# The last six lower products of an MLP stage issued as twelve of 256 columns

## Chip, cores and metric

The kernel runs on one core of one Trainium2 chip. The metric is the device time of one execution in microseconds (us). The kernel before was timed three times: 345.19 us is the median, 344.91 and 346.03 are the ends. Times within a run are read from one profiled execution.

## What is computed

A decoder block on 256 tokens of width 1024, all in float32: a gated mixer (causal pooling and attention), and then an MLP with a squared ReLU. The change lies in the MLP, which holds the last half of the time:

```python
u2 = rmsnorm(h, norm_mlp_pre[l])
a = jnp.square(jax.nn.relu(u2 @ w_up[l]))          # 1024 -> 4096
h = h + rmsnorm(a @ w_down[l], norm_mlp_post[l])   # 4096 -> 1024
```

## The kernel before

Every float32 operand of a product is split into a high part of type float32r and a low part, the rest (`split_hi` L87 on ScalarE, `split_lo` L91 on VectorE or GpSimd). A product of two operands is then three TensorE products: high by high, high by low, low by high. Each of them is a weight load of a 128x128 block (the stationary operand, read by PEld in the profile) and a stream of 256 or 512 columns (the moving operand, PE in the profile) that adds into a bank of PSUM. A bank holds 512 float32 columns.

The hidden width of 4096 is cut into eight chunks of 512. For each chunk there is an **upper part** and a **lower part**:

- The upper part of chunk j (`up_half` L794, called twice) computes `u2 @ w_up` for 512 hidden units. The weights `up_h`, `up_l` are stationary; the tokens `u2h`, `u2l` move, 256 columns at a time. Each call of `up_half` issues 2 x 8 x 3 = 48 products through `mm3` (L223; its three products are L227, L228 and L229), so an upper part has 96 products of 256 columns. Squared ReLU and the split of its result into `ah`, `al` follow on ScalarE and VectorE.
- The lower part of chunk j multiplies that result by the chunk's 512 rows of `w_down`. Here the tokens `ah`, `al` are stationary and the weights `dn_h`, `dn_l` move, 512 columns at a time. `mm3_wide` (L231) issues six products for one token tile t and one block k of 128 rows: for each of two banks the high tokens by `dn_h` (L236) and by `dn_l` (L237), and then for both banks the low tokens by `dn_h` (L240). Two token tiles and four blocks make 8 x 6 = 48 products of 512 columns. They accumulate in the four banks `pd` over all chunks.

The order on TensorE is written out by hand in program order; nothing reorders it. Upper parts 0 and 1 come first. In upper part 1 each call of `up_half` stands behind four 128x128 transposes (`up_turned`, tile `ut_ps`). Then the loop at L870 runs over j: lower part j, the splits of the next blocks of weights (`split_next(2)` L876), and upper part j + 2 while there is one. So the order is lower 0, upper 2, lower 1, upper 3, ..., lower 5, upper 7, lower 6, lower 7. Six upper parts (2 to 7) stand directly behind a lower part; lower 6 is followed by lower 7. `finish` (L844) ends each token tile.

Other stretches of the program matter for comparison, since they too consist of products of 256 columns through `mm3`: the feature products of the mixer (tiles `q_ps`, `k_ps`, `p_ps`, `g_ps`, 48 products per bank), the scores (`s_ps`, L512 and L513), the pooling projection (`y_ps`, six products a time) and the two branch products (`bp_ps` and `ba_ps`, 24 products a time, turn by turn, L701).

Of the kernel before, what the change touches and what calls it, by code (L numbers as in the profile page):

```python
# [17 lines left out]
D = 1024  # L18
S = 256
NT = S // P  # L20
# [13 lines left out]
def hybrid_block(ctx: ExitStack, tc: tile.TileContext, x, norm_mix_pre, w_in, b_gate, pool_w, pool_scale,  # L34
# [4 lines left out]
    nc = tc.nc  # L39
# [10 lines left out]
    def bank(name):  # L50
        return psum.tile([P, 512], F32, tag="bank", name=name)
# [83 lines left out]
    bu, bd = [None] * NCH, [None] * NCH  # L135
# [18 lines left out]
    def split_next(n=1):  # L154
        for _ in range(n):
            if done[1] < len(order):
                b = next_block()
                b.split(b in shared)
                load_next()
# [71 lines left out]
    def mm3_wide(pss, xhl, whl, start, stop):  # L231

        (xh, xl), (wh, wl) = xhl, whl
        for n, ps in enumerate(pss):
            c = slice(n * 512, (n + 1) * 512)
            nc.tensor.matmul(ps, xh, wh[:, c], start=start, stop=False, skip_group_check=True)  # L236
            nc.tensor.matmul(ps, xh, wl[:, c], start=False, stop=False, skip_group_check=True)  # L237
        for n, ps in enumerate(pss):
            c = slice(n * 512, (n + 1) * 512)
            nc.tensor.matmul(ps, xl, wh[:, c], start=False, stop=stop, skip_group_check=True)  # L240

    def tokens(hl, k, t):
        c = slice(t * P, (t + 1) * P)
        return hl[0][:, k, c], hl[1][:, k, c]

    def wide(blocks, k):
        b = blocks[k // 2]
        return b.hi[:, k % 2, :], b.lo[:, k % 2, :]
# [478 lines left out]
    def out_proj(t, ks, pss, n=None):  # L727
        for k in ks:
            if n is None:
                mm3_wide(pss, tokens(m, k, t), wide(bo, k), k == 0, k == KD - 1)  # L730
            else:
                h, l = wide(bo, k)
                c = slice(n * 512, (n + 1) * 512)
                mm3(pss[n], tokens(m, k, t), (h[:, c], l[:, c]), k == 0, k == KD - 1)
# [36 lines left out]
    def up_parts(j):  # L771
        return tuple(work.tile([P, 4, S], F32R, tag=f"a{i}", name=f"a{i}{j}") for i in "hl")
# [21 lines left out]
    def up_half(j, f2, a):  # L794
        ps = bank(f"up_ps{j}_{f2}")
        for i in range(2):
            cs = slice((2 * f2 + i) * P, (2 * f2 + i + 1) * P)
            for k in range(KD):
                mm3(ps[:, i * S:(i + 1) * S], narrow(bu[j], k, cs), (u2[0][:, k, :], u2[1][:, k, :]),
                    k == 0, k == KD - 1)  # L800
        if f2 == 0:
            split_next(2)
        q = two(squared_relu(ps, f"{j}_{f2}"))
        parts(a[0][:, 2 * f2:2 * f2 + 2, :], a[1][:, 2 * f2:2 * f2 + 2, :], q)
# [36 lines left out]
    pd = [[bank(f"d_ps{t}{n}") for n in range(2)] for t in range(NT)]  # L841
# [27 lines left out]
    prev, nxt = a0, a1  # L869
    for j in range(NCH):  # L870
        last = j == NCH - 1
        for t, k in [(t, k) for t in range(NT) for k in range(4)]:
            if last and t == NT - 1:
                continue
            mm3_wide(pd[t], tokens(prev, k, t), wide(bd[j], k), j == 0 and k == 0, last and k == 3)
        split_next(2)  # L876
        if last:
            break
        if j + 2 < NCH:
            a = up_parts(j + 2)  # L880
            up_half(j + 2, 0, a)
            up_half(j + 2, 1, a)
        else:
            a = None
        prev, nxt = nxt, a
# [35 lines left out]
```

## Time and profile before

| what | us |
|---|---|
| median of three runs | 345.19 |
| the profiled execution | 345.76 |
| its span, from the first to the last instruction | 344.0 |
| PE busy in the span | 334.4 |
| lower part 0, from 181.23 to 192.13 | 10.90 |
| upper part 2, from 192.13 to 203.44 | 11.31 |
| lower part 1, from 203.44 to 214.31 | 10.87 |

The rows of a timeline have the start in us, the duration in us, the engine, the line, the operation and its operands as output<-inputs, sizes, and a count where rows are merged. Inputs of a matmul are named in an order that does not tell which one moves. The durations of products overlap: a product of 256 columns is shown with 0.28 us and one of 512 columns with 0.39 us, while the next one starts long before that has passed. What a product costs in a dense stream is therefore read from the distance of two starts, which is called the **pitch** here. In a view of windows, each row has the stretch, its length, and the busy time of each engine in it, with the number of instructions that touch it in brackets.

### The profile page before, as it was taken

Reading aid. Unit: us, or ns where it says so; the run is one execution under the profiler, and the core shown is the slowest. Engines: PE = TensorE matmul, PEld = TensorE weight load, DVE = VectorE, ACT = ScalarE, POOL = GpSimd, SP = SyncE. Lnnn points to the kernel's source line nnn. Section 1 sums busy time; section 2 is a strip of 40 time slices with the busy share of each in tenths; the row PEclk is TensorE's granted clock in tenths of the full one; section 3 lists DMA queues with packets and bytes.
Section 4 is the critical chain, followed back from the end, with each engine's and each line's share of the span. In section 5 each row is a group of like instructions: output and inputs, shape, how many; then the busy total and the mean of one; then the engine's idle time right before and its main releaser. Section 6 shows DMA issues by size and latency. Waiting matters only on the chain.

```text
span 344.0 us, 5679 instructions
## 1 busy us (share of the span) xinstructions
PE 334.4 (97%) x2313; PEld 309.1 (90%) x2313; DVE 220.5 (64%) x288; ACT 182.3 (53%) x257; POOL 77.3 (22%) x70
## 2 busy tenths in 40 slices
PE   7999999999999999999999999999999999999991
PEld 6799999999999999888898998989989889899880
DVE  2899698996476689376677736547366373653545
ACT  3895658765656755175767435354273451644231
POOL 3699965144303000046600000000000000000000
PEclk9999999999999999999999999999999999999998
DMA  6988761654455946707364854908539166090003
GB/s 203 386 283 282 165 229 32 231 160 157 174 177 193 364 131 229 253 2 245 122 189 179 310 180 163 325 2 274 216 100 328 62 247 243 35 327 9 0 0 122
DMA packets 27506, 63.04 MB, mean 183 GB/s; under 512 B 1332, under 2 KB 3160, under 8 KB 27480
## 3 DMA queue, kind: packets, MB, share of 16 engines
q1 hardware_dynamic: 26904, 62.15, 52.3%
q0 software_dynamic: 576, 0.52, 1.0%
q8 instruction: 18, 0.29, 0.4%
q14 instruction: 8, 0.07, 0.1%
HBM read 61.10 MB, written 1.05 MB: 181 GB/s over the span
## 4 chain that ended last, share of the span: by engine, by line
PE 93%; DVE 2%; DMA 2%; ACT 2%; SPq 0%; issue 0%; DVEq 0%; ACTq 0%
PE up_ps L227 9%; PE up_ps L229 9%; PE up_ps L228 9%; PE d_ps L236 8%; PE d_ps L237 8%; PE d_ps L240 8%; PE g_ps L227 4%; PE g_ps L228 4%; PE g_ps L229 4%; PE wo_ps L236 2%; PE wo_ps L240 2%; PE wo_ps L237 2%; DMA x_sb<-in_x_dram 2%; PE q_ps L227 1%; PE bp_ps L228 1%; PE bp_ps L227 1%
## 5 line engine op out<-in xcount | busy, mean ns | idle before, releaser
L227 PE MATMUL up_ps<-u2h,up_h 128*128 128x256 f32 x224 | 63.0, 281 | 0.0
L228 PE MATMUL up_ps<-u2l,up_h 128*128 128x256 f32 x224 | 62.8, 280 | 0.0
L229 PE MATMUL up_ps<-u2h,up_l 128*128 128x256 f32 x224 | 62.8, 280 | 0.0
L93 DVE TENSOR_TENSOR dn_l<-dn_r,dn_h 128x2048 fp32r<-128x2048 f32 x16 | 36.5, 2291 | 16.5 <-ACT dn_h L89 16.4
L236 PE MATMUL d_ps<-dn_h,ah 128*128 128x512 f32 x120 | 46.7, 389 | 0.0
L237 PE MATMUL d_ps<-dn_l,ah 128*128 128x512 f32 x120 | 46.7, 389 | 0.0
L229 PEld LDWEIGHTS up_ps<-u2h,up_l 128*128 128x128 f32 x224 | 42.9, 191 | 0.0
L228 PEld LDWEIGHTS up_ps<-u2l,up_h 128*128 128x128 f32 x224 | 42.1, 188 | 0.2
L227 PEld LDWEIGHTS up_ps<-u2h,up_h 128*128 128x128 f32 x224 | 42.1, 188 | 0.2
L89 ACT ACTIVATE dn_h<-dn_r 128x2048 fp32r<-128x2048 f32 x16 | 30.4, 1914 | 21.4 <-issue 12.8
L863 POOL TENSOR_TENSOR o_out<-o_out,g_mlp_post 128x256 f32<-128x256 f32 x2 | 1.5, 729 | 165.5 <-DVE rr L295 161.4
L240 PE MATMUL d_ps<-dn_h,al 128*128 128x512 f32 x120 | 36.9, 389 | 0.0
L227 PE MATMUL g_ps<-uh,g_h 128*128 128x256 f32 x128 | 36.1, 282 | 0.0
L228 PE MATMUL g_ps<-ul,g_h 128*128 128x256 f32 x128 | 35.7, 279 | 0.0
L229 PE MATMUL g_ps<-uh,g_l 128*128 128x256 f32 x128 | 35.7, 279 | 0.0
L93 DVE TENSOR_TENSOR up_l<-up_r,up_h 128x2048 fp32r<-128x2048 f32 (+1 forms) x14 | 30.2, 2193 | 8.1 <-ACT up_h L89 8.1
L776 ACT ACTIVATE relu<-up_ps 128x512 f32<-128x512 f32 x16 | 9.5, 594 | 41.5 <-PE up_ps L229 41.5
L778 DVE TENSOR_TENSOR a<-up_ps,relu 128x512 f32<-128x512 f32 x16 | 11.0, 690 | 30.9 <-ACT relu L776 30.8
L89 ACT ACTIVATE up_h<-up_r 128x2048 fp32r<-128x2048 f32 x16 | 29.9, 1904 | 1.6 <-PE wo_ps L240 1.6
L240 PEld LDWEIGHTS d_ps<-dn_h,al 128*128 128x128 f32 x120 | 22.5, 188 | 4.7
L237 PEld LDWEIGHTS d_ps<-dn_l,ah 128*128 128x128 f32 x120 | 22.5, 188 | 4.4
L236 PEld LDWEIGHTS d_ps<-dn_h,ah 128*128 128x128 f32 x120 | 22.5, 188 | 4.4
(225 smaller groups left out, 836.7 us busy)
## 6 DMA issues: line engine op xcount, KB each, us to landing
up_r<-in_w_up_dram SPq DMA_DIRECT2D x16, 1024.0 KB, 5.6
dn_r<-in_w_down_dram SPq DMA_DIRECT2D x16, 1024.0 KB, 5.5
g_r<-in_w_in_dram SPq DMA_DIRECT2D x8, 1024.0 KB, 5.5
o_r<-in_w_out_dram SPq DMA_DIRECT2D x4, 1024.0 KB, 4.8
v_r<-in_w_in_dram SPq DMA_DIRECT2D x8, 256.0 KB, 5.7
q_r<-in_w_in_dram SPq DMA_DIRECT2D x4, 512.0 KB, 6.2
k_r<-in_w_in_dram SPq DMA_DIRECT2D x2, 1024.0 KB, 5.5
p_r<-in_w_in_dram SPq DMA_DIRECT2D x2, 1024.0 KB
```

Of the source, the lines that this page charges most:

```text
L89: nc.scalar.activation(self.hi[:, s, :], self.raw[:, s, :], AF.Copy)
L93: eng.tensor_tensor(self.lo[:, s, c], self.raw[:, s, c], self.hi[:, s, c].bitcast(F32), ALU.subtract)
L227: nc.tensor.matmul(ps, wh, rh, start=start, stop=False, skip_group_check=True)
L228: nc.tensor.matmul(ps, *second, start=False, stop=False, skip_group_check=True)
L229: nc.tensor.matmul(ps, *third, start=False, stop=stop, skip_group_check=True)
L236: nc.tensor.matmul(ps, xh, wh[:, c], start=start, stop=False, skip_group_check=True)
L237: nc.tensor.matmul(ps, xh, wl[:, c], start=False, stop=False, skip_group_check=True)
L240: nc.tensor.matmul(ps, xl, wh[:, c], start=False, stop=stop, skip_group_check=True)
L776: nc.scalar.activation(r, ps, AF.Relu)
L778: nc.vector.tensor_tensor(a, ps, r, ALU.mult)
L863: nc.gpsimd.tensor_tensor(o[:, 768:D], o[:, 768:D], g_mlp_post[:, 768:D], ALU.mult)
```

## The change

In lower parts 0 to 6, the last of the eight calls of `mm3_wide` (token tile 1, block 3) is replaced by a new function, `mm3_quarters`. It covers the same columns with the same operands in pieces of 256 columns: for each of four pieces the high tokens by `dn_h` and by `dn_l`, and then for the four pieces the low tokens by `dn_h`.

```diff
+    def mm3_quarters(pss, xhl, whl):
+
+        (xh, xl), (wh, wl) = xhl, whl
+        pieces = [(pss[c // 512][:, c % 512:c % 512 + 256], slice(c, c + 256)) for c in range(0, D, 256)]
+        for ps, c in pieces:
+            nc.tensor.matmul(ps, xh, wh[:, c], start=False, stop=False, skip_group_check=True)
+            nc.tensor.matmul(ps, xh, wl[:, c], start=False, stop=False, skip_group_check=True)
+        for ps, c in pieces:
+            nc.tensor.matmul(ps, xl, wh[:, c], start=False, stop=False, skip_group_check=True)
...
         for t, k in [(t, k) for t in range(NT) for k in range(4)]:
             if last and t == NT - 1:
                 continue
-            mm3_wide(pd[t], tokens(prev, k, t), wide(bd[j], k), j == 0 and k == 0, last and k == 3)
+            if not last and (t, k) == (NT - 1, 3):
+
+                mm3_quarters(pd[t], tokens(prev, k, t), wide(bd[j], k))
+            else:
+                mm3_wide(pd[t], tokens(prev, k, t), wide(bd[j], k), j == 0 and k == 0, last and k == 3)
```

On TensorE, at the seam between lower part 0 and upper part 2, the order before is this (numbers in names tell buffers and banks apart; `d_ps` are the lower banks, `up_ps` an upper bank):

```order
L236 MATMUL d_ps_2195<-dn_2_h,ah_1733 128x512
L237 MATMUL d_ps_2195<-dn_2_l,ah_1733 128x512
L236 MATMUL d_ps_2196<-dn_2_h,ah_1733 128x512
L237 MATMUL d_ps_2196<-dn_2_l,ah_1733 128x512
L240 MATMUL d_ps_2195<-dn_2_h,al_1734 128x512
L240 MATMUL d_ps_2196<-dn_2_h,al_1734 128x512
L227 MATMUL up_ps_0_2260<-u2h,up_0_h 128x256
L228 MATMUL up_ps_0_2260<-u2l,up_0_h 128x256
L229 MATMUL up_ps_0_2260<-u2h,up_0_l 128x256
```

The same place on TensorE after the change:

```order
L247 MATMUL d_ps_2195<-dn_2_h,ah_1733 128x256
L248 MATMUL d_ps_2195<-dn_2_l,ah_1733 128x256
L247 MATMUL d_ps_2195<-dn_2_h,ah_1733 128x256
L248 MATMUL d_ps_2195<-dn_2_l,ah_1733 128x256
L247 MATMUL d_ps_2196<-dn_2_h,ah_1733 128x256
L248 MATMUL d_ps_2196<-dn_2_l,ah_1733 128x256
L247 MATMUL d_ps_2196<-dn_2_h,ah_1733 128x256
L248 MATMUL d_ps_2196<-dn_2_l,ah_1733 128x256
L250 MATMUL d_ps_2195<-dn_2_h,al_1734 128x256 x2
L250 MATMUL d_ps_2196<-dn_2_h,al_1734 128x256 x2
L227 MATMUL up_ps_0_2266<-u2h,up_0_h 128x256
L228 MATMUL up_ps_0_2266<-u2l,up_0_h 128x256
```

Nothing moved: six rows became twelve products in the same place (the last two rows stand for two products each), and the upper part now stands behind products of 256 columns. The seventh place, the end of lower part 6 on TensorE, has no upper part behind it; after the change it reads:

```order
L247 MATMUL d_ps_2196<-dn_26_h,ah_3024 128x256
L248 MATMUL d_ps_2196<-dn_26_l,ah_3024 128x256
L250 MATMUL d_ps_2195<-dn_26_h,al_3025 128x256 x2
L250 MATMUL d_ps_2196<-dn_26_h,al_3025 128x256 x2
L236 MATMUL d_ps_2193<-dn_28_h,ah_3214 128x512
L237 MATMUL d_ps_2193<-dn_28_l,ah_3214 128x512
```

There the twelve pieces are followed by the products of 512 columns of lower part 7. The other engines and the DMA queues have the same instructions in the same order as before.

## Prediction

> **What bounds the kernel now.** The page comes first: the span, the busy times, and the chain that ended last; then the view of waits for TensorE alone.
>
> ```profile
> span 344.0 us, 5679 instructions
> PE 334.4 (97%) x2313; PEld 309.1 (90%) x2313; DVE 220.5 (64%) x288; ACT 182.3 (53%) x257; POOL 77.3 (22%) x70
> PE 93%; DVE 2%; DMA 2%; ACT 2%; SPq 0%; issue 0%; DVEq 0%; ACTq 0%
> ```
>
> ```profile
> PE x_ps L306 <- DMA x_sb<-in_x_dram: 1.0, 1, 1.0
> PE busy L61 <- PEq L907: 0.8, 1, 0.8
> ```
>
> 93% of the chain is TensorE, and its only listed waits (1.0 and 0.8 us) lie at the start of the program. So the MLP costs what its products cost, each at its pitch, and every nanosecond of pitch goes straight into the time. The windows of the MLP show the parts one by one: the second call of upper part 1, lower part 0, upper part 2, lower part 1.
>
> ```profile
> 175.68:181.23 5.55, 5.55 (x51) 5.55 (x50) 4.85 (x4) 2.67 (x5) 0.00 (x0) 1.00 0.56 185
> 181.23:192.13 10.90, 10.90 (x51) 9.02 (x49) 8.56 (x15) 7.96 (x10) 0.00 (x0) 1.00 0.48 163
> 192.13:203.44 11.31, 11.31 (x98) 11.31 (x97) 5.40 (x4) 3.15 (x3) 0.00 (x0) 1.00 0.91 329
> 203.44:214.31 10.87, 10.87 (x50) 9.01 (x49) 6.40 (x5) 6.75 (x5) 0.00 (x0) 1.00 0.32 106
> ```
>
> PE is busy for the whole of each, at granted clock 1.00. Lower part 1 is 48 products in 10.87 us: 226.5 ns each. Upper part 2 is 96 products in 11.31 us: 117.8 ns each. The 48 products of the second call in upper part 1 took 5.55 us, 115.6 ns each, though they have the same shape, the same tokens and the same kind of weights. The timeline says why: the first rows below are the end of that call, then the start of lower part 0.
>
> ```profile
> 179.87 0.28 PE L227 MATMUL up_ps<-u2h,up_h 128*128 128x256 f32 x1
> ...
> 181.23 0.39 PE L236 MATMUL d_ps<-dn_h,ah 128*128 128x512 f32 x1
> ...
> 182.16 0.39 PE L240 MATMUL d_ps<-dn_h,al 128*128 128x512 f32 x1
> ```
>
> From 179.87 to 181.23 stand twelve products: 1.36 us, or **113.3 ns** each, half of the 226.5 of a product with twice the columns. Upper part 2 never gets there; its rows begin behind the last two lower products:
>
> ```profile
> 191.68 0.61 PE L240 MATMUL d_ps<-dn_h,al 128*128 128x512 f32 x2
> 192.13 0.28 PE L227 MATMUL up_ps<-u2h,up_h 128*128 128x256 f32 x1
> 192.25 0.28 PE L228 MATMUL up_ps<-u2l,up_h 128*128 128x256 f32 x1
> 192.36 0.28 PE L229 MATMUL up_ps<-u2h,up_l 128*128 128x256 f32 x1
> ...
> 203.32 0.28 PE L229 MATMUL up_ps<-u2h,up_l 128*128 128x256 f32 x1
> 203.44 0.39 PE L236 MATMUL d_ps<-dn_h,ah 128*128 128x512 f32 x1
> ```
>
> From the first row to the last it keeps 117 to 118 ns, as do the other five that follow a lower part. So a dense stream of 256 columns has **two steady pitches, 113.3 and 117.8 ns**, and which one holds is decided where the stream begins. The transposes ahead of upper part 1 let it in at the fast one; products of 512 columns let it in at the slow one, six times out of six. DMA traffic does not separate them, as the four windows in the next fence show: fast at 294 and 404 GB/s, slow at 111 and 298.
>
> **The change part by part.** What decides is how a 256-column stream begins when another stands ahead of it without a gap. The mixer has such seams. First windows: `g_ps` behind scores, `g_ps` behind the pooling projection, `ba_ps` behind `bp_ps`, `bp_ps` behind `ba_ps` (48, 48, 24 and 24 products); then the seam of the third of these in the timeline.
>
> ```profile
> 59.01:64.47 5.46, 5.46 (x51) 1.00 0.94 294
> 94.94:100.60 5.66, 5.66 (x51) 1.00 0.38 111
> 115.45:118.18 2.73, 2.73 (x26) 1.00 1.02 404
> 118.18:121.01 2.83, 2.83 (x27) 1.00 0.75 298
> ```
>
> ```profile
> 115.34 0.28 PE L229 MATMUL bp_ps<-yh,bp_l 128*128 128x256 f32 x1
> 115.45 0.28 PE L227 MATMUL ba_ps<-oTh,ba_h 128*128 128x256 f32 x1
> 115.57 0.28 PE L228 MATMUL ba_ps<-oTl,ba_h 128*128 128x256 f32 x1
> 115.69 0.28 PE L229 MATMUL ba_ps<-oTh,ba_l 128*128 128x256 f32 x1
> 115.80 0.28 PE L227 MATMUL ba_ps<-oTh,ba_h 128*128 128x256 f32 x1
> 115.91 0.28 PE L228 MATMUL ba_ps<-oTl,ba_h 128*128 128x256 f32 x1
> ```
>
> That is 113.8, 117.9, 113.8 and 117.9 ns each: `ba_ps` changes from the long pitch to the short one within three products (2.73 us against 24 x 113.3 = 2.72: 0.01 us to settle), and `g_ps` behind scores at 5.46 against 48 x 113.3 = 5.44 (0.02). I counted all fifteen such seams in the timeline: seven lead to 113.3 (scores behind `k_ps`, `p_ps` behind scores, `g_ps` behind scores, and all four `ba_ps`), eight to 117.8 or more (`g_ps` and `y_ps` behind each other twice each, `bp_ps` four times). Of the three kinds that were slow ahead of the seam and whose follower also runs fast somewhere, two went fast (`ba_ps`; `g_ps` behind scores) and one stayed slow (`g_ps` behind `y_ps`).
>
> *Removed and added.* Seven calls lose 6 products of 226.5 ns (1.36 us) and get 12 of 256 columns, with 6 more weight loads each. A load stands beside the product ahead of it: in the lower windows PEld is busy 9.02 of 10.90 us, in the upper ones throughout, and PE is without a gap in both. At 113.3 ns the twelve cost 1.36 us: nothing lost. At 117.8 ns, 1.41: 0.05 a call. The slowest dense rows of this shape are the six of `y_ps` and the scores ahead of `g_ps`:
>
> ```profile
> 57.01 0.36 PE L512 MATMUL s_ps<-stacked 128*128 128x256 f32 x1
> 59.01 0.29 PE L227 MATMUL g_ps<-uh,g_h 128*128 128x256 f32 x1
> ...
> 100.60 0.28 PE L227 MATMUL y_ps<-ys_pws 128*128 128x256 f32 x1
> ...
> 101.32 0.28 PE L227 MATMUL g_ps<-uh,g_h 128*128 128x256 f32 x1
> ```
>
> `y_ps` is 6 in 0.72 us, 120 ns each; at that, the twelve cost 1.44, or 0.08 a call. Seven calls: 0 to +0.57 us. I take 117.8, the row nearest to it, since 256 columns directly behind 512 have run so six times: **+0.38 us**.
>
> The Trainium skill speaks against pieces: Perfetto Trace Analysis, section Matmuls, says that larger matmuls are more efficient than smaller ones. TensorE: Matmul & The Clock Gate, section Back-to-back issue gap, puts the warm gap at N / 2.4 + 2.5 ns; by that, an estimate from the page, each of 42 halved products would cost 2.5 ns more, 0.11 us in all. Here 2 x 113.3 against 226.5 shows no such fixed cost at the short pitch, and 2 x 117.8 a larger one (9 ns) at the long one.
>
> *Upper parts 2 to 7.* At the fast pitch: 96 x 113.3 = 10.88 us, plus 0.02 to settle, plus the way back into 512 columns: the four products from 181.23 to 182.16 took 0.93 us against 4 x 226.5 = 0.91, another 0.02, which lower parts 1 to 6 would now pay. 11.31 − 10.92 = 0.39 us, six times: **−2.34 us**.
>
> *The other engines* keep their order. A shorter upper part is only worth its time if the next weights are split by then. Rows of VectorE, and the PE row that they must be ahead of:
>
> ```profile
> 207.52 4.50 DVE L93 TENSOR_TENSOR up_l<-up_r,up_h 128x2048 fp32r<-128x2048 f32 x2 [1.11 <-ACT up_h L89]
> 214.31 0.28 PE L227 MATMUL up_ps<-u2h,up_h 128*128 128x256 f32 x1
> 216.69 2.29 DVE L93 TENSOR_TENSOR dn_l<-dn_r,dn_h 128x2048 fp32r<-128x2048 f32 x1 [0.60 <-ACT dn_h L89]
> 225.62 0.39 PE L236 MATMUL d_ps<-dn_h,ah 128*128 128x512 f32 x1
> ```
>
> `up_l` is ready at 212.02, 2.3 us early, and hangs on the end of the upper part before, with a whole lower part between, which does not shrink. `dn_l` is ready at 218.98, 6.6 us early. 0.39 us a stage uses neither up, so nothing new becomes late.
>
> The sum is 0.38 − 2.34 = −1.96 us: from the profiled execution's 345.76 us (1.76 us of it outside the span) to 343.8, and from the median of 345.19, which lies 0.57 below it, to **343.2 us**.
>
> **The rivals.**
> 1. *The upper parts stay slow.* For it: `g_ps` behind `y_ps`, and six of six behind lower parts; the pitch could hang on what the lower products leave behind, whatever their width. Against it: `ba_ps`, four of four. Then only the twelve pieces count, 0 to +0.57: 345.2 to 345.8 us. A rule of the Trainium skill gives this too: SBUF — State Buffer, section Who interferes with whom, has the moving operand and the weight load on independent read ports, and TensorE waiting on nobody; with nothing to collide, there are no two pitches. That one shape with the same operands shows 113.3 and 117.8 speaks against that much of it.
> 2. *Slower: the pieces bring in a third pitch.* The scores at 57.01 are 16 in 2.00 us, 125 ns with their first gap, and `y_ps` 120. If upper parts inherited 120 ns, they would cost 6 x 96 x 2.2 = +1.27, with the twelve at 120 +1.84: 347.0 us. It counts as slower from a pitch of 118.6 on (0.57 + 576 x 0.8 ns = 1.03). Against it: neither follower, `g_ps` behind scores or behind `y_ps`, kept 120.
> 3. *Some stages only.* If half of the upper parts, or half of each, run fast: 0.38 − 1.17 = −0.8, 344.4 us. Against it: all six seams have been alike so far, and the buffers repeat from stage to stage.
>
> The change does what it says: the order on TensorE has the twelve products in all seven places.
>
> **How the numbers follow.** Fast upper parts 0.48, rival 1 0.38, rival 2 0.08, rival 3 0.06. A measurement tells about 0.3%, 1.04 us, from no change. Faster by more: 0.48 (the forecast, 344.15 or less, with a little of rival 3 for what misses it). Within: rival 1, the rest of rival 3, a little of rival 2: 0.45. Slower: 0.07. The range takes in the forecast with free pieces (−2.34: 342.9), rival 3 and rival 1 with its dear end (345.8), and 0.3 to 0.4 us for the spread of the runs at both ends: 342.5 to 346.1. The forecast's own range is 342.5 to 343.8.
>
> **What would show it.** In the windows, six upper parts of 10.9 us instead of 11.31, with a pitch of 113 from about the fourth product, and lower parts from 10.87 to 10.94. If the twelve pieces show 113, the +0.38 was wrong; if 120, it is 0.57. If the upper parts stay at 11.31, the seam argument fell, and `y_ps` was the right likeness. A wait of PE ahead of an upper part would break the claim on the other engines.

## The result and the profile after

The change took 343.66 us (median of 5 runs, 342.96 to 344.09) against 345.19 before (now also 5 runs, 344.91 to 346.03). The two medians differ by 1.53 us, a ratio of 0.9956. The ratio estimated from all runs is 0.9943 with a 95% interval of 0.9930 to 0.9957, which is 1.5 to 2.4 us. The profiled execution went from 345.76 to 343.66 us, its span from 344.0 to 341.9. First the page of the changed kernel, the rows that answer to those of before:

```profile
span 341.9 us, 5763 instructions
PE 332.6 (97%) x2355; PEld 308.6 (90%) x2355; DVE 220.7 (65%) x288; ACT 182.8 (53%) x257; POOL 77.3 (23%) x70
```

There are 42 more products and 42 more weight loads than before, and TensorE is busy for 1.8 us less. The windows of the changed kernel say where: the 42 whole products of lower part 0, its twelve pieces, upper part 2, the 42 whole products of lower part 1, and, in the last row, the twelve pieces of lower part 6. The columns after the stretch are its length, PE's busy time, the granted clock, the DMA share and GB/s; the other engines are left out.

```profile
180.95:190.48 9.53, 9.53 (x44) 1.00 0.46 139
190.48:191.92 1.44, 1.44 (x14) 1.00 0.75 302
191.92:202.81 10.89, 10.89 (x98) 1.00 0.94 339
202.81:212.35 9.54, 9.54 (x44) 1.00 0.21 62
321.68:323.12 1.44, 1.44 (x14) 1.00 0.00 0
```

Upper part 2 fell from 11.31 to 10.89 us. The twelve pieces take 1.44 us, 120 ns each, where six whole products took 1.36. The timeline of the changed kernel at that seam:

```profile
190.48 0.28 PE L247 MATMUL d_ps<-dn_h,ah 128*128 128x256 f32 x1
190.60 0.28 PE L248 MATMUL d_ps<-dn_l,ah 128*128 128x256 f32 x1
190.72 0.28 PE L247 MATMUL d_ps<-dn_h,ah 128*128 128x256 f32 x1
...
191.44 0.64 PE L250 MATMUL d_ps<-dn_h,al 128*128 128x256 f32 x4
191.92 0.29 PE L227 MATMUL up_ps<-u2h,up_h 128*128 128x256 f32 x1
192.04 0.28 PE L228 MATMUL up_ps<-u2l,up_h 128*128 128x256 f32 x1
192.16 0.28 PE L229 MATMUL up_ps<-u2h,up_l 128*128 128x256 f32 x1
192.27 0.28 PE L227 MATMUL up_ps<-u2h,up_h 128*128 128x256 f32 x1
192.39 0.28 PE L228 MATMUL up_ps<-u2l,up_h 128*128 128x256 f32 x1
```

The reader is to see the pitch: 0.12 through the pieces, 0.12 for the first two products of the upper part, and then 0.11 and 0.12 in turn, which is 113.3 on the average: (202.81 − 192.39) / 92 = 113.3 ns. All six upper parts look the same.

The sum over the trace: from the start of lower part 0 to the start of lower part 6 the profiled executions took 314.37 − 181.23 = 133.14 us before and 312.15 − 180.95 = 131.20 after, −1.94 us; lower part 6 gives back some 0.1; and lower part 0 started 0.28 us earlier, which has nothing to do with the change, since nothing ahead of it differs. So the change is worth 1.8 us by the trace. That lies inside the measured interval of 1.5 to 2.4 us.

### The profile page after: what moved, and what is told of

Read it like the earlier page. It is cut to its first block, busy times and chain, and to the rows that moved or that the text cites. A ratio compares the mean times of both kernels' runs of the same rounds, so it can differ in the third digit from the quotient of the medians.

```text
span 341.9 us, 5763 instructions
## 1 busy us (share of the span) xinstructions
PE 332.6 (97%) x2355; PEld 308.6 (90%) x2355; DVE 220.7 (65%) x288; ACT 182.8 (53%) x257; POOL 77.3 (23%) x70
## 4 chain that ended last, share of the span: by engine, by line
PE 84%; DVE 5%; DMA 4%; ACT 2%; SPq 1%; POOL 1%; issue 1%; DVEq 0%; ACTq 0%; POOLq 0%
PE up_ps L227 9%; PE up_ps L228 9%; PE up_ps L229 9%; PE d_ps L237 7%; PE d_ps L236 7%; PE d_ps L240 7%; PE g_ps L227 4%; PE g_ps L228 4%; PE g_ps L229 4%; DMA v_r<-in_w_in_dram 2%; PE wo_ps L240 2%; PE wo_ps L236 2%; PE wo_ps L237 2%; DMA k_r<-in_w_in_dram 2%; DVE k_l L93 1%; PE bp_ps L228 1%
## 5 line engine op out<-in xcount | busy, mean ns | idle before, releaser
L227 PE MATMUL up_ps<-u2h,up_h 128*128 128x256 f32 x224 | 62.1, 277 | 0.0
L228 PE MATMUL up_ps<-u2l,up_h 128*128 128x256 f32 x224 | 61.9, 276 | 0.0
L229 PE MATMUL up_ps<-u2h,up_l 128*128 128x256 f32 x224 | 61.9, 276 | 0.0
L229 PEld LDWEIGHTS up_ps<-u2h,up_l 128*128 128x128 f32 x224 | 42.1, 188 | 0.0
L236 PE MATMUL d_ps<-dn_h,ah 128*128 128x512 f32 x106 | 41.3, 390 | 0.0
L237 PE MATMUL d_ps<-dn_l,ah 128*128 128x512 f32 x106 | 41.3, 390 | 0.0
L240 PE MATMUL d_ps<-dn_h,al 128*128 128x512 f32 x106 | 32.6, 389 | 0.0
L93 POOL TENSOR_TENSOR up_l<-up_r,up_h 128x640 fp32r<-128x640 f32 (+1 forms) x4 | 15.6, 3909 | 46.7 <-ACT up_h L89 46.7
L227 PEld LDWEIGHTS g_ps<-uh,g_h 128*128 128x128 f32 x128 | 24.3, 190 | 0.0
L228 PEld LDWEIGHTS g_ps<-ul,g_h 128*128 128x128 f32 x128 | 24.1, 188 | 0.0
```

Of the source, the lines that this page charges most:

```text
L93: eng.tensor_tensor(self.lo[:, s, c], self.raw[:, s, c], self.hi[:, s, c].bitcast(F32), ALU.subtract)
L227: nc.tensor.matmul(ps, wh, rh, start=start, stop=False, skip_group_check=True)
L228: nc.tensor.matmul(ps, *second, start=False, stop=False, skip_group_check=True)
L229: nc.tensor.matmul(ps, *third, start=False, stop=stop, skip_group_check=True)
```

## Experiments

The theory at the outset: a dense stream of 256-column products takes up 113.3 or 117.8 ns at its first products, by what stands directly ahead. The rivals: that pieces anywhere do it, that any disturbance at the seam does it, and, added after the first four runs, that the pitch follows from where the two operands lie in memory. Most of these kernels were executed once, beside one execution of the kernel before; for them the windows are the better evidence. The stretch from the first `q_ps` to the first `g_ps` has the same code in all thirteen traces and took between 38.38 and 39.25 us in them, so two single times can differ by up to 0.9 us for that alone.

**Pieces one block earlier.**

```diff
-            if not last and (t, k) == (NT - 1, 3):
+            if not last and (t, k) == (NT - 1, 2):
```

> The twelve pieces of 256 columns stand one block earlier (token tile 1, block 2), and the last block of each lower part is six products of 512 columns again, directly ahead of the upper part. Theory (the pitch of an upper part is set by what stands directly ahead of it): the pieces cost 120 ns as in the change, the upper parts are back at 117.8 ns, 11.31 us each; with 0.03 us more for the way back into 512 columns the MLP costs 7 x 0.11 = 0.8 us more than in the kernel before. Rival (pieces anywhere in the lower part put the stream into another rhythm that lasts): upper parts of 10.9 us as in the change.

Measured: 346.82 against 345.40 us, 1.4 more where 0.8 was expected; from the start of lower part 0 on, its trace is 0.7 us longer than that of the kernel before. Windows of this run: the pieces, the six whole products behind them, and upper part 2.

```profile
189.73:191.16 1.43, 1.43 (x13) 1.00 0.51 57
191.16:192.55 1.39, 1.39 (x8) 1.00 0.83 327
192.55:203.86 11.31, 11.31 (x98) 1.00 0.90 325
```

The gain is gone, the cost stays: six products of 512 columns in between are enough to bring back 11.31 us. So in this kernel it is the products directly ahead that count, not pieces anywhere in the lower part.

**Only the last two products, and only the last one, in pieces.** In both, lower part 6 keeps its whole products. The last one alone:

```diff
+        whole = [(pss[n], slice(n * 512, (n + 1) * 512)) for n in range(2)]
...
-        for ps, c in pieces:
+        for ps, c in whole:
             nc.tensor.matmul(ps, xh, wh[:, c], start=False, stop=False, skip_group_check=True)
             nc.tensor.matmul(ps, xh, wl[:, c], start=False, stop=False, skip_group_check=True)
-        for ps, c in pieces:
+        for ps, c in whole[:1] + pieces[2:]:
...
-            if not last and (t, k) == (NT - 1, 3):
+            if j + 2 < NCH and (t, k) == (NT - 1, 3):
```

> Only the last two products of lower parts 0 to 5 (low tokens by high weights) are cut, into four pieces of 256 columns; lower part 6 keeps 512 columns. Theory (256 columns directly ahead are enough, however few): the upper parts take 10.9 us, and a lower part costs about 0.02 us over six whole products instead of 0.07; 0.3 us in all below the change. Rival (a run of some ten pieces is needed, or the alternation of high and low weights in the first eight): upper parts stay at 117.8 ns, 11.31 us, about the time of the kernel before.

> Only the very last product of lower parts 0 to 5 is cut, into two pieces of 256 columns. Theory (what stands directly ahead, however short): upper parts of 10.9 us with next to no cost in the lower part. Rival (the first pieces run at 113 ns still, as the first of the twelve did in the change, and only the slow pieces shift the rhythm): with two pieces there is one slow one at most, and upper parts stay at 117.8 ns.

Measured: 342.98 and 342.75 us against 345.40. Both had upper parts of 10.90 us. Windows with the last one alone: 47 whole products, two pieces, upper part 2.

```profile
180.50:191.17 10.67, 10.67 (x49) 1.00 0.48 156
191.17:191.40 0.23, 0.23 (x3) 1.00 1.04 427
191.40:202.30 10.90, 10.90 (x98) 1.00 0.94 339
```

Two pieces of 0.23 us do what twelve did. Ten of the twelve pieces only cost 0.07 us a stage.

**An extra narrow product at the seam**, in the kernel before:

```diff
         ps = bank(f"up_ps{j}_{f2}")
+        if j > 1 and f2 == 0:
+            nc.tensor.matmul(ps[:, 0:P], narrow(bu[j], 0, slice(0, P))[0], u2[0][:, 0, 0:P], start=True, stop=False,
+                             skip_group_check=True)
```

> The kernel before, with one extra product of 128 columns ahead of upper parts 2 to 7, whose result the first product of the upper part overwrites; the lower parts keep 512 columns. Theory (any short disturbance at the seam, in which the weight load is longer than the product, lets the upper part settle at the short pitch, as the transposes ahead of upper part 1 did): upper parts of 10.9 us plus some 0.11 us for the extra product, about 1.8 us below the kernel before. Rival (256-column lower products themselves are needed): 117.8 ns stays, and the time rises by 6 x 0.11 = 0.7 us.

Measured: 346.01 against 345.40 us. The timeline of this run at the seam:

```profile
191.56 0.22 PE L797 MATMUL up_ps<-u2h,up_h 128*128 128x128 f32 x1
191.62 0.33 PE L227 MATMUL up_ps<-u2h,up_h 128*128 128x256 f32 x1
191.79 0.28 PE L228 MATMUL up_ps<-u2l,up_h 128*128 128x256 f32 x1
191.91 0.28 PE L229 MATMUL up_ps<-u2h,up_l 128*128 128x256 f32 x1
```

The rhythm is broken (0.06, then 0.17), and the products behind it are back at 0.12: 96 products and the extra one took 11.42 us. The theory as I had put it here was wrong: this disturbance is not enough.

**Moving the upper part's tokens in memory.** Addresses can be read from the built program. Call *distance* the start of the stationary operand minus that of the moving one, modulo 256 bytes. Before the change it is 64 for upper parts 1 to 7, for `g_ps` and for `ba_ps`, 192 for `bp_ps`, and 0 for `y_ps`, for the lower part and so for its pieces. (Upper part 0 is issued otherwise than the others: 48 products of 512 columns in which the tokens are stationary, at a distance of 192.) Three runs of the kernel before, without pieces, move `u2` alone by 64, 128 and 192 bytes; the first of them:

```diff
+    work.tile([P, 16], F32, name="gap", bufs=1)
     u2 = tuple(work.tile([P, KD, S], F32R, name=f"u2{i}", bufs=1) for i in "hl")
 
-    work.tile([P, 16], F32, name="gap", bufs=1)
```

> The kernel before with the 64-byte gap allotted ahead of the tokens u2 instead of behind them: u2 lies 64 bytes higher, all else stays. In the built program the moving u2 then starts at the same offset modulo 256 bytes as the stationary weights of the upper part, as the moving and stationary operands of y_ps and of the lower pieces do, which run at 120 ns. Theory (the pitch of a dense 256-column stream follows from the distance of its two operands in memory, modulo some power of two, and only at a distance of 64 bytes does it depend on what stands ahead): upper parts 1 to 7 run at 120 ns throughout, upper part 1 too, which costs 6 x 0.21 + 0.6 = 1.9 us over the kernel before. Rival (the pitch is set at the seam alone): 113.3 in upper part 1, 117.8 in the others, as before.

> The kernel before with u2 128 bytes higher (the lower part's operands keep their offsets modulo 256): weights and u2 are then at the distance, modulo 256 bytes, of bp_ps, which runs at 117.8 ns four times of four. Theory (distance): all upper parts at 117.8 ns, part 1 included, 0.4 us over the kernel before. Rival (seam alone): part 1 at 113.3, the others at 117.8, no change.

> The kernel before with u2 192 bytes higher: a distance of 128 bytes modulo 256, which no dense stream of the kernel has. Theory (distance): one pitch in all upper parts whatever stands ahead; if it is 113.3, 2.4 us below the kernel before without any pieces, if it is 117.8 to 120, 0.4 to 1.9 us above. Rival (seam alone): no change.

Measured: 347.97, 345.86 and 347.96 us against 344.84. Windows of each run in turn: the second call of upper part 1 (48 products, behind transposes) and upper part 2 (96 products, behind 512 columns).

```profile
176.19:182.02 5.83, 5.83 (x51) 1.00 0.62 199
192.93:204.44 11.51, 11.51 (x97) 1.00 0.84 303
```

```profile
175.32:181.06 5.74, 5.74 (x51) 1.00 0.61 193
191.98:203.29 11.31, 11.31 (x98) 1.00 0.85 313
```

```profile
176.12:181.89 5.77, 5.77 (x51) 1.00 0.62 196
192.77:204.29 11.52, 11.52 (x98) 1.00 0.80 305
```

At distance 0 both are slow: 11.51 / 96 = 119.9 ns behind 512 columns, and no 113.3 behind transposes, where the kernel before had it. At 192 both are at 117.8. At 128 the pitch swings from product to product: 117 to 123 ns in turn in upper part 2, 120.0 on the average, and 115 to 122 in the call behind transposes, 118.6 without its first product. So the seam makes no difference at 0 and 192 and a small one at 128; of the four distances, only 64 has shown both 113.3 and 117.8. The same three runs moved upper part 0 as well: its first 18 products of 512 columns took 4.13 us at distance 192 in the kernel before, and then 4.09 at 0, 4.20 at 64 and 4.19 at 128.

The single times rose more than the windows (by 3.1 us at distance 0). The spans of the two traces, 346.2 against 344.0, differ by 2.2: upper parts 1 to 7 give 1.8, and 0.5 comes from the stretch ahead of the first `g_ps`, which the edit does not touch; the rest nearly cancels.

**Pieces at the upper part's distance.** The last product of lower parts 0 to 5 in two pieces, and the gap behind `u2` doubled, so that `ah`, `al` lie 64 bytes higher and lower and upper parts have the same distance. The whole products of the lower part move to that distance too:

```diff
-    work.tile([P, 16], F32, name="gap", bufs=1)
+    work.tile([P, 32], F32, name="gap", bufs=1)
```

> The kernel with the last product of lower parts 0 to 5 in two pieces, and the gap behind u2 128 bytes instead of 64, so that the tokens ah, al of the lower parts lie 64 bytes higher against the weights that move. Pieces and upper part then have the same distance of operands. Theory (the pieces help because at their distance they run at 120 ns, which the upper part cannot keep and leaves for 113.3): with this distance the pieces behave as an upper part does behind 512 columns, at 117.8 ns from the first, and the upper parts stay at 117.8, 11.31 us. Rival (any 256-column products of the lower part ahead will do): upper parts of 10.9 us as before.

Measured: 346.21 against 344.84 us. Windows of this run: the whole products of lower part 0, upper part 2, those of lower part 1, upper parts 3 and 4.

```profile
180.35:191.31 10.96, 10.96 (x49) 1.00 0.50 161
191.54:202.85 11.31, 11.31 (x98) 1.00 0.87 314
202.85:213.82 10.97, 10.97 (x49) 1.00 0.31 109
214.06:224.96 10.90, 10.90 (x98) 1.00 0.76 271
236.15:247.46 11.31, 11.31 (x98) 1.00 0.74 262
```

Neither side had this: the upper parts are slow, fast, slow, fast, slow, fast, although the code is the same each time. Of the two distances tried, the pieces helped at all six seams only at 0. And the whole products of 512 columns became slower: 10.96 / 47 = 233 ns instead of 226.7. In these runs a 512-column stream was fastest at distance 0, a 256-column stream at 64.

At distance 64 the 512-column products take 231 and 236 ns in turn. Ahead of the three slow upper parts the last two of them took 231 and then 236, ahead of the three fast ones 236 and then 231. So what is handed on may be a phase of that rhythm; no run tests this.

The mixer shows the same thing in code that neither kernel changes: one code, two outcomes. The windows of two of its `g_ps` stretches (48 products behind transposes, and 48 behind `o_ps`), first in the kernel before, then in the run with the pieces one block earlier:

```profile
74.03:79.77 5.74, 5.74 (x52) 1.00 0.91 324
82.36:87.89 5.53, 5.53 (x50) 1.00 0.76 234
```

```profile
74.33:79.89 5.56, 5.56 (x52) 1.00 0.95 341
82.48:88.22 5.74, 5.74 (x51) 1.00 0.63 207
```

Nothing ahead of these stretches differs between the two kernels, and yet the fast and the slow one have changed places. So at distance 64 the kind of product directly ahead does not settle the pitch by itself.

**Timed: the short version, and two predictions from the distance elsewhere.** The kernel with the last product in two pieces was timed alone, then with the operand of `bp_ps` moved to distance 64, and then with that of `y_ps` moved there too.

```diff
-            yp.extend(placed(mixer, NG, t, t[2:], a) for t, a in (("q_yh", 0), ("k_yl", 16)))
+            yp.extend(placed(mixer, NG, t, t[2:], a) for t, a in (("q_yh", 32), ("k_yl", 48)))
...
-    ys_pws = mixer.tile([P, 2, NG, S + P], F32R, tag="prob", name="ys_pws")
-    ys = [ys_pws[:, i, :, 0:S] for i in range(2)]
-    pws = [ys_pws[:, i, :, S:S + P] for i in range(2)]
+    ys_pws = mixer.tile([P, 8 * (S + P) + 64], F32R, tag="prob", name="ys_pws")
+    ys = [ys_pws[:, i * NG * S:(i + 1) * NG * S].rearrange("p (g s) -> p g s", g=NG) for i in range(2)]
+    at_pw = 8 * S + 16
+    pws = [ys_pws[:, at_pw + i * NG * P:at_pw + (i + 1) * NG * P].rearrange("p (g c) -> p g c", g=NG) for i in range(2)]
```

> The kernel with only the last product of lower parts 0 to 5 in two pieces, timed. From the windows of its first look: lower plus upper part 21.80 us against 22.19 before and 21.87 in the change, so 6 x 0.39 = 2.3 us below the kernel before (342.8 us), 0.6 us below the change.

> As the kernel before this one, and the pooled operand of bp_ps moved in memory by 128 bytes, so that it stands 64 bytes below the weights modulo 256, as ba_ps has it; nothing else moves. Theory (distance decides, and at 64 bytes a stream behind a fast one stays fast): the four bp_ps stretches, slow four times of four so far, take 2.72 us instead of 2.83, at least the three behind ba_ps; 0.3 to 0.4 us. Rival (bp_ps is slow because of what it stands behind): 2.83 us as before.

> As the kernel before this one, and the operands of y_ps laid out so that they too stand 64 bytes apart. Theory: y_ps behind a fast g_ps runs at 113 ns instead of 120, and the 144 products of g_ps behind it (slow so far) stay fast: 12 x 6.7 + 144 x 4.4 ns = 0.7 us more, 1.1 us below the version without the two moves, about 341.7 us. Rival (g_ps is slow there for another reason): y_ps alone changes, 0.1 us.

| kernel | us, median | ratio to before (345.56), 95% |
|---|---|---|
| two pieces a stage | 343.29 | 0.9936, 0.9910 to 0.9961 |
| and `bp_ps` at 64 | 343.58 | 0.9940, 0.9925 to 0.9956 |
| and `y_ps` at 64 | 341.45 | 0.9887, 0.9870 to 0.9904 |

The first was expected at 342.8 us and is not told apart from the change by its time (0.9943 there); the windows give it 0.07 us a stage. The second missed: `bp_ps` did not become fast. Its windows, the 96 products of `g_ps` ahead, `bp_ps`, and `ba_ps` behind it:

```profile
101.40:112.70 11.30, 11.30 (x99) 1.00 0.61 207
112.70:115.53 2.83, 2.83 (x27) 1.00 1.05 398
115.53:118.36 2.83, 2.83 (x27) 1.00 0.98 375
```

Now `ba_ps`, which took 2.73 us before, is at 2.83 too. `g_ps` hands 117.7 ns on, and with all three at distance 64 nothing changes it any more. So the move alone cost 0.4 us in the windows. The third kernel is the same with a `y_ps` that no longer disturbs; its windows are one `y_ps` (six products), the 48 of `g_ps` behind it, the 96 of `g_ps` ahead of `bp_ps`, `bp_ps` and `ba_ps`:

```profile
93.15:93.83 0.68, 0.68 (x8) 1.00 0.00 0
93.83:99.27 5.44, 5.44 (x50) 1.00 0.36 86
99.95:110.83 10.88, 10.88 (x98) 1.00 0.75 266
110.83:113.55 2.72, 2.72 (x26) 1.00 1.03 353
113.55:116.27 2.72, 2.72 (x26) 1.00 1.02 340
```

Everything from `y_ps` to the last `ba_ps` runs at 113.3 ns; a fast `g_ps` (113.3) stands at the head of the chain. In these two kernels a stream at distance 64 keeps the pitch that it is handed by a stream at the same distance, the short one as well as the long one. Behind a stream at another distance it need not: before the change, `ba_ps` left the 117.8 of `bp_ps`, at 192, for 113.3. It was expected at 341.7 us and took 341.45, 4.1 us below the kernel before, and it beats the change by more than their intervals.

## Why the prediction came true

- **Fast upper parts, −2.34 us.** Right, in direction and size: 10.89 to 10.90 us against the 10.92 that I had with the way back included. The 0.02 for the way back into 512 columns shows as 9.54 us for 42 whole products instead of 42 x 226.7 = 9.52. No wait of PE arose ahead of any upper part.
- **The pieces, +0.38 us.** Mis-sized. I took 117.8 ns, "the row nearest to it, since 256 columns directly behind 512 have run so six times". They ran at 120 ns behind a first one at 113, on the average 119.4, so a call cost 0.07 us more than six whole products and seven calls 0.51. With the way back into 512 columns, lower parts 1 to 5 took 10.97 us where I had 10.94. The right likeness was `y_ps`, whose operands have the pieces' distance of 0. The twelve behind which no upper part stands, in lower part 6, were pure loss.
- **The ground for the seam.** Here there was luck. I counted seams by their outcome, seven of fifteen, and gave fast upper parts 0.48. The count was too coarse: `y_ps` at distance 0 and `bp_ps` at 192 were in it, and at these distances every stream came to the same pitch whatever stood ahead. The forecast did not ask where the operands lie, and the pieces happened to lie at 0; in the kernel with the doubled gap, where they and the whole products lay at 64, only three upper parts of six were fast. Nor is the pitch always settled where a stream begins, as I had it: in the kernel before, `p_ps` changed its own after a pause (see the last section). That a 256-column stream ahead is what matters was right for the pieces here (pieces a block earlier lose the gain), but its cause was not told: neither the width (pieces at distance 64 worked for every other upper part) nor the one disturbance that was tried (the narrow product) is enough.
- **Rival 1**, upper parts that stay slow, is what pieces one block earlier, or an ill-placed operand, give. The Trainium skill's rule behind it (SBUF — State Buffer, section Who interferes with whom: moving operand and weight load have independent read ports, TensorE waits on nobody) does not carry over to the pitch: 64 bytes on one operand moved upper part 2 from 117.8 to 119.9 ns and upper part 1 from 113.3 to 120, with the same products in the same order. Why the placement counts, the runs do not show.
- **Rival 2**, a third pitch of 120 for the upper parts, exists, but at distance 0 and not by inheritance: `up_ps` behind pieces of 120 ns left that pitch within two products.
- **Rival 3**, some stages only, did not occur in the change; it is what the kernel with the doubled gap did, in three stages of six.
- **The remainder.** By windows the change gives 1.8 us, by the sum 1.96, and the median 1.53. The sum is 0.13 too high for the price of the pieces; the rest lies within the spread of the runs (1.1 us from lowest to highest).

What the runs show is that the products directly ahead and the placement of the operands both bear on the pitch. The two `g_ps` stretches that changed places show that this is not all of it, and why either counts stays open. One case stays open in particular: `y_ps` and the pieces have the same distance and the same 120 ns, yet `g_ps` behind `y_ps` settled at 117.8 and the upper part behind the pieces at 113.3. No run tells these two seams apart.

## What to carry to other kernels

Where TensorE runs without gaps, read the distance of starts, stretch by stretch, and not the busy share: PE was busy at 97% before and after. If products of one shape run at two pitches, look at where the two operands lie relative to each other and at what stands directly ahead. In the last kernel the placement of two stretches gave 1.8 us by the medians (1.2 by the windows) on top of the 2.3 of the pieces, and cost no instruction. Move all stretches of a chain and measure: `bp_ps` moved alone cost 0.4 us. If a seam is to be changed, try the last product only; here two pieces did what twelve did.

## What was not expected of the hardware

- The pitch of 256-column float32r products depended on the distance of their operands modulo 256 bytes: 120 ns at 0, 113.3 or 117.8 at 64, 117.8 at 192, and at 128 swinging between 115 and 123 with 118.6 or 120 on the average. This holds for streams with one distance throughout; the scores, which have 64 and 192 in turn, took 113.3 ns at one place of the kernel before and 120 at another. For 512 columns it was 226.7 ns at 0 and 231 to 236 (233 on the average) at 64.
- At a distance of 64 bytes either pitch lasted through stretches at that distance without a pause: in the kernel with `bp_ps` moved, 288 products from the last `g_ps` to the last `ba_ps` at 117.7 to 117.8 ns, in the next one the same 288 at 113.3. Across a pause it could change: in the kernel before, the first `p_ps` stretch ran at 113 ns from 44.20 to 45.67 us, paused for 0.3 us, and went on at 118 from 46.24 to 50.12.
